# The transfers of the linear attention's first weights go behind the last tile of x

## The chip, the cores and the metric

The kernel runs on one core of one Trainium2 chip. The metric is the device time of one execution in microseconds (us): the median of the runs before is 1082.19 us, of three (1080.2 to 1083.65).

## The reference, cut to what matters

One decoder layer over 1024 tokens of width 1024, in float32:

```
h     = rmsnorm(x)
proj  = h @ w_in          # q, k, v and the indexer's iq, ik, iw of the sparse attention;
                          # q, k, v, gate rank and output gate of the linear attention
o_a   = sparse attention: per query the 256 keys with the best indexer score
        score = sum_h relu(iq_h . ik) * iw_h, then softmax over those keys
o_b   = gated linear attention in chunks of 64, RMSNorm and swish gate
x     = x + concat(o_a, o_b) @ w_out
x     = x + MoE(rmsnorm(x))   # 4 groups of 8 experts, top group, top 2 experts in it
```

Only the start of this is touched: reading x, the indexer's projection and scores, and the first part of the linear attention's projection.

## The kernel before, in words

The 1024 tokens are eight tiles of 128. TensorE works in a reduced float32 format, so each operand is held as two parts, a rounded one (hi) and what is left over (lo), and each product is three matmuls (`project_steps`, line 268). Three parts of the start matter here.

`prepare(t)` (line 287) fetches tile t of x by one transfer on SP's queue into one of three slots (tag "big", also used by the score tiles `rl` and the constants `craw`). TensorE transposes it in two halves (line 295), VectorE scales each half out of PSUM (line 298), ScalarE rounds it (line 299) and VectorE takes the rest (line 300). ScalarE squares and sums the tile (line 302) for the norm. A slot is free again when the transposes and the squares have read it.

The indexer: its weights are loaded first (`w_idx`, line 309). Projection t (24 matmuls of 312 columns) is read by ScalarE (`index_evac`, line 331), and `index_operands` (line 334) makes keys and queries of it with VectorE (lines 332 to 351), TensorE's transposes (lines 341 and 356) and ScalarE (lines 342 and 357). The scores of tile t (line 382) are evacuated by ScalarE (line 383) and added up by VectorE (line 387). The first score matmuls, of tile 2, stand in TensorE's order behind the operands of tile 3.

`load_w` (line 250) fetches weights of one group of 384 columns: four pairs of K blocks, each pair into one of three raw slots by one transfer for each piece of columns. Of each block ScalarE makes the rounded part (line 262) and GpSimd or VectorE the rest (line 263). `qkv_load(0)` has three pieces of 128 columns, so twelve transfers of 128 KB, and all its splits on GpSimd (`BY_QKV`). It is called in `filler` (line 453), whose matmuls fill TensorE's time between the score matmuls; the indexer's projections 4 to 7 come first in it, then the linear attention's q, k, v of all tiles, then `vr_load(0)` and its projection.

TensorE's order from the scoring on is the order of the program. The other engines' queues, and SP's, are ordered by a planner: it plays the program through on estimated times and issues what is ready, earlier program text first. So transfers late in the text, such as those of `qkv_load(0)`, are issued while earlier ones wait for a slot.

Of the kernel before, what the change touches and what calls it, by code (L numbers as in the profile page):

```python
# [22 lines left out]
P = 128  # L23
# [111 lines left out]
def layer(ctx, tc, x, norm1_g, w_in, q_norm_g, k_norm_g, rel_bias, gla_gate_w2, gla_gate_b, gla_out_norm_g, w_out,  # L135
          norm2_g, w_router_group, b_router_group, w_router_expert, b_router_expert, w_exp_gate, w_exp_up,
          w_exp_down, con, out):
    nc = tc.nc
    V, A, G, T = nc.vector, nc.scalar, nc.gpsimd, nc.tensor

    def f32(ap):
        return ap.bitcast(F32)
# [11 lines left out]
    def ps_tp():  # L154
        return psum.tile([P, 4, P], F32, tag="tp", name="tp", bufs=n_tp)
# [7 lines left out]
    def rsqrt(pool, y, ss, scale, bias, n, eng=None):  # L163

        e = eng or V
        u = pool.tile([P, n], F32, name="rs_u", tag=f"rs_u{n}")
        w = pool.tile([P, n], F32, name="rs_w", tag=f"rs_w{n}")
        A.activation(w, ss, AF.Ln, scale=scale, bias=eps[bias])
        A.activation(w, w, AF.Exp, scale=-0.5)
        if eng:  # L170
            e.tensor_scalar(u, ss, -0.5 * scale, -0.5 * bias, op0=OP.mult, op1=OP.add)
            e.tensor_tensor(u, u, w, op=OP.mult)
            e.tensor_tensor(u, u, w, op=OP.mult)
        elif n == 1:
            V.tensor_scalar(u, ss, -0.5 * scale, -0.5 * bias, op0=OP.mult, op1=OP.add)
            V.scalar_tensor_tensor(u, w, u, w, op0=OP.mult, op1=OP.mult)
        else:
            V.scalar_tensor_tensor(u, ss, bias / scale, w, op0=OP.add, op1=OP.mult)
            V.scalar_tensor_tensor(u, u, -0.5 * scale, w, op0=OP.mult, op1=OP.mult)
        if eng:  # L180
            e.tensor_scalar(u, u, 1.5, None, op0=OP.add)
            e.tensor_tensor(y, w, u, op=OP.mult)
        else:
            V.scalar_tensor_tensor(y, u, 1.5, w, op0=OP.add, op1=OP.mult)
# [32 lines left out]
    def two_parts(t):  # L217

        pool = hold[HOLD[t]]
        if HOLD[t] % 2:  # L220
            return [pool.tile([P, D], F32R, name="w4", tag="w4") for _ in range(2)]
        w = pool.tile([P, 2, D], F32R, name="w8", tag="w8")
        return [w[:, 0], w[:, 1]]
# [26 lines left out]
    def load_w(pieces, pool=None, width=384, by="GGGGGGGG"):  # L250
        wh, wl = [], []
        for kk in range(0, KC, 2):
            raw = wp.tile([P, 2, 384], F32, tag="wr", name="wr", bufs=3)[:, :, :width]
            o = 0
            for c, n in pieces:
                nc.sync.dma_start(raw[:, :, o:o + n],
                                  w_in[0, kk * P:(kk + 2) * P, c:c + n].rearrange("(k p) c -> p k c", p=P))
                o += n
            for k in range(2):
                a = (pool or wp).tile([P, width], F32R, tag=f"wh{kk + k}" if pool else "wh", name="wh")  # L260
                b = (pool or wp).tile([P, width], F32R, tag=f"wl{kk + k}" if pool else "wl", name="wl")
                A.activation(a, raw[:, k], AF.Copy)  # L262
                (V if by[kk + k] == "V" else G).tensor_tensor(b, raw[:, k], f32(a), op=OP.subtract)  # L263
                wh.append(a)
                wl.append(b)
        return wh, wl

    def project_steps(t, w, done, width=384):

        wh, wl = w  # L270
        ps = ps_pj()
        for k in range(KC):
            hh, hl = hT[t][0][:, k], hT[t][1][:, k]
            for i, (x_, y_) in enumerate(((hh, wh), (hh, wl), (hl, wh))):
                T.matmul(ps[:, :width], x_, y_[k], start=(k == 0 and i == 0), stop=(k == KC - 1 and i == 2))  # L275
                if k == KC - 1 and i == 2:
                    done(ps)
                yield width * 0.43

    def project(t, w, width=384):  # L280
# [2 lines left out]
            pass  # L283
        return out_[0]


    def prepare(t):
        xt = idp.tile([P, D], F32, name="xt", tag="big", bufs=3)
        nc.sync.dma_start(xt, x[0, t * P:(t + 1) * P])
        hT.append([w.rearrange("p (k t) -> p k t", k=KC) for w in two_parts(t)])  # L290
        sq = idp.tile([P, D], BF, name="sq", tag="sq", bufs=1)
        for hf in range(2):
            tp = ps_tp()
            for k in range(4):
                T.transpose(tp[:, k], xt[:, (hf * 4 + k) * P:(hf * 4 + k + 1) * P], ident)
            hi, lo = (hT[t][i][:, hf * 4:hf * 4 + 4] for i in range(2))
            xs = idp.tile([P, 4, P], F32, name="xs", tag="xs")
            V.tensor_tensor(xs, tp, g1[:, hf * 4:hf * 4 + 4, None].to_broadcast([P, 4, P]), op=OP.mult)
            A.activation(hi, xs, AF.Copy)
            V.tensor_tensor(lo, xs, f32(hi), op=OP.subtract)  # L300
        c = slice(t, t + 1)
        A.activation(sq, xt, AF.Square, accum_out=ssq[:, c])
        rsqrt(idp, rstd[:, c], ssq[:, c], 1.0 / D, EPS, 1, G)
        G.tensor_scalar(nrstd[:, c], rstd[:, c], -1.0, None, op0=OP.mult)

    with nc.allow_non_contiguous_dma("small parameter"):
        nc.sync.dma_start(g1, norm1_g[0].rearrange("(k p) -> p k", p=P))
    prepare(0)
    w_idx = load_w([(IQ, 296), (GLR, 16)], w1p, 312, "VVVVVVVV")
    prepare(1)  # L310
# [18 lines left out]
    def index_evac(t, pj):  # L329
        pr = prs[t] = idp.tile([P, 312], F32, name="pr", tag="pr")  # L330
        A.activation(pr, pj[:, :312], AF.Copy, scale=rstd[:, t:t + 1])
        V.tensor_scalar(iww[:, t], pr[:, 288:296], 0.0625, None, op0=OP.mult)

    def index_operands(t):
        pr = prs[t]
        k4 = idp.tile([P, 2, 2, 32], F32R, name="k4", tag="k4")
        ikb = pr[:, None, 256:288].to_broadcast([P, 2, 32])
        V.tensor_copy(k4[:, :, 0], ikb)
        V.tensor_tensor(k4[:, :, 1], ikb, f32(k4[:, :, 0]), op=OP.subtract)
        tp = ps_mm().rearrange("p (a t) -> p a t", a=4)  # L340
        T.transpose(tp[:, 0], f32(k4.rearrange("p a b d -> p (a b d)")), ident)
        A.activation(k4T[:, t * P:(t + 1) * P], tp[:, 0], AF.Copy)
        G.tensor_copy(glr[:, t], pr[:, 296:312])
        if t < 2:
            return
        q4 = idp.tile([P, 8, 2, 2, 32], F32R, name="q4", tag="q4", bufs=1)
        iqb = pr[:, 0:256].rearrange("p (h d) -> p h d", h=8)
        for j in range(2):
            V.tensor_copy(q4[:, :, 0, j], iqb)
        for j in range(2):  # L350
            V.tensor_tensor(q4[:, :, 1, j], iqb, f32(q4[:, :, 0, 0]), op=OP.subtract)
        q4T = idp.tile([P, 8, P], F32R, name="q4T", tag="q4T", bufs=3)
        for hf in range(2):
            tp = ps_mm().rearrange("p (a t) -> p a t", a=4)
            for h in range(4):
                T.transpose(tp[:, h], f32(q4[:, hf * 4 + h].rearrange("p a b d -> p (a b d)")), ident)
            A.activation(q4T[:, hf * 4:hf * 4 + 4], tp, AF.Copy)
        q4Ts[t] = q4T
# [36 lines left out]
    def qkv_load(p):  # L395
        c = p * P
        return load_w([(QB + c, P), (KB + c, P), (VB + 2 * c, P)], by=BY_QKV[p])

    def vr_load(p):
        c = p * P  # L400
        return load_w([(VB + 2 * c + P, P), (RG + 2 * c, 2 * P)], by=BY_VR[p])

    def evac_qkv(p, t, pj):
        gq[p, t] = gqp.tile([P, 384], F32, name="gq", tag="gq", bufs=9)
        A.activation(gq[p, t], pj[:, :384], AF.Copy, scale=rstd[:, t:t + 1])
# [17 lines left out]
    for t in range(2, NT):  # L423
        prepare(t)
# [18 lines left out]
    def filler():  # L443

        for t in range(4, NT):
            for ns in project_steps(t, w_idx, lambda ps: index_evac(t, ps), 312):
                yield ns, 0
            if t > 4:
                index_operands(t - 1)
                yield 1000, t - 1  # L450
        p1c.close()
        pools["gvp"] = p2.enter_context(tc.tile_pool(name="gvp", bufs=1, side="right"))
        w = qkv_load(0)
        for t in range(NT):
            for ns in project_steps(t, w, lambda ps: evac_qkv(0, t, ps)):
                yield ns, 0
            if t == 0:
                index_operands(NT - 1)
                yield 1000, NT - 1
        w = vr_load(0)  # L460
        for t in range(NT):
            for ns in project_steps(t, w, lambda ps: evac_vr(0, t, ps)):
                yield ns, 0
# [318 lines left out]
    w = qkv_load(1)  # L782
# [18 lines left out]
    w = vr_load(1)  # L801
# [764 lines left out]
    for i, (kind, e) in enumerate(plan):  # L1566
# [8 lines left out]
        x = xs.pop(e)  # L1575
# [19 lines left out]
    with tc.If(nov > CAP):  # L1595
# [5 lines left out]
        with tc.For_i(0, NE, 1) as e:  # L1601
# [7 lines left out]
            x, parts = {}, []  # L1609
# [51 lines left out]
```

## Time and profile before

| what | value |
|---|---|
| median of the runs | 1082.19 us |
| the profiled execution | 1076.3 us, span 1074.5 us |
| mean granted TensorE clock | 0.965 |
| busy in the span | PE 92%, DVE 71%, ACT 63%, POOL 36% |

PE is TensorE, PEld its weight loads, DVE VectorE, ACT ScalarE, POOL GpSimd; SPq is SyncE's queue, which issues transfers. The profile covers one execution. In its rows L12 is line 12 of the kernel, "wr<-in_w_in" means that tile wr is written from w_in, and x3 that three such instructions are merged. The granted clock is a share of full speed: 1.00 is 2.4 GHz and 0.50 is 1.2 GHz.

### The profile page before, as it was taken

To read this page: it belongs to the slowest core of one execution; us is meant where nothing else is said; L and a number is where in the kernel's file an instruction comes from. 1 tells how busy PE (TensorE), PEld (TensorE's weight loads), DVE (VectorE), ACT (ScalarE), POOL (GpSimd) and SP (SyncE) were. 2 spreads that over 40 slices of the span, in tenths; PEclk is the share of its full clock that TensorE was granted. 3 is DMA by queue.
4 is the path that set the end of the run, shared out by engine and by line. 5 is a ranking of instruction groups with operands and counts; after the bars stand their busy time and mean duration, and the time that the engine had idled before them with its cause. 6 is when DMAs were issued, how large, how long until landed. Compare 5 with 4: busy or idle time off the path is not lost.

```text
span 1074.5 us, 17967 instructions
## 1 busy us (share of the span) xinstructions
PE 990.3 (92%) x5839; PEld 803.9 (75%) x5839; DVE 764.2 (71%) x2037; ACT 674.0 (63%) x1662; POOL 382.2 (36%) x499
## 2 busy tenths in 40 slices
PE   7799989999998999999989999949999999999892
PEld 7789878878887988988977878836666666666561
DVE  6877898684775566767765666656887778888771
ACT  7688755365555666666755533427777777777660
POOL 4510325551413225245332201254435444443421
PEclk9899989999999999999999999968999999999996
DMA  8220202020202102012131379769999999999983
GB/s 251 81 60 1 60 1 70 11 70 21 70 11 70 38 9 65 10 51 79 58 93 48 126 255 381 292 223 286 318 317 320 326 327 324 333 316 324 341 281 46
DMA packets 83206, 170.88 MB, mean 159 GB/s; under 512 B 14856, under 2 KB 45760, under 8 KB 82976
## 3 DMA queue, kind: packets, MB, share of 16 engines
q1 hardware_dynamic: 75936, 148.01, 40.8%
q0 software_dynamic: 7168, 21.65, 9.4%
q8 instruction: 48, 0.79, 0.3%
q14 instruction: 54, 0.44, 0.1%
HBM read 148.23 MB, written 26.88 MB: 163 GB/s over the span
## 4 chain that ended last, share of the span: by engine, by line
PE 59%; DMA 14%; DVE 14%; ACT 7%; issue 3%; POOL 2%; SPq 1%; POOLq 0%; ACTq 0%; DVEq 0%
PE pj L275 19%; DMA out_dram<-y,idx 10%; PE pj L1138 8%; PE mm L1512 3%; PE po L964 3%; PE pj L1463 3%; PE pj L1464 3%; PE pj L1465 3%; PE tp L952 2%; DVE w L1386 2%; PE mm L1159 1%; PE mm L936 1%; PE tp L1473 1%; PE mm L711 1%; PE mm L935 1%
## 5 line engine op out<-in xcount | busy, mean ns | idle before, releaser
L275 PE MATMUL pj<-wh,w 128*128 128x384 f32 (+1 forms) x1152 | 322.9, 347 | 6.0 <-DVE gv L415 5.0
L275 PEld LDWEIGHTS pj<-wh,w 128*128 128x128 f32 x1152 | 211.4, 193 | 13.8 <-DVE gv L415 5.6
L1385 ACT ACTIVATE w<-w 128x512 fp32r<-128x512 f32 x320 | 192.0, 628 | 46.0 <-PE mm L1465 27.5
L1386 DVE TENSOR_TENSOR w<-w,w 128x512 fp32r<-128x512 f32 x283 | 187.2, 698 | 31.7 <-ACT w L1385 28.3
L275 PE MATMUL pj<-wl,w 128*128 128x384 f32 (+1 forms) x576 | 199.3, 346 | 1.5 <-POOL wl L263 1.1
L275 PEld LDWEIGHTS pj<-wl,w 128*128 128x128 f32 x576 | 111.8, 194 | 4.7 <-POOL wl L263 1.3
L1463 PE MATMUL pj<-w,xT 128*96 128x512 f32 x256 | 105.5, 412 | 0.6 <-ACT w L1385 0.5
L1464 PE MATMUL pj<-w,xT 128*96 128x512 f32 x256 | 101.9, 398 | 2.3 <-DVE w L1386 1.2
L1465 PE MATMUL pj<-w,xT 128*96 128x512 f32 x256 | 101.7, 397 | 0.0
L1138 PE MATMUL pj<-w,mhl 128*128 128x512 f32 x384 | 101.1, 404 | 0.0
L929 POOL TENSOR_TENSOR cb<-bt,maskb 128x256 f32<-128x256 f32 (+1 forms) x64 | 43.5, 682 | 122.1 <-DVE mx L940 103.4
L1537 POOL DMA_INDIRECT out_dram<-y,idx x30 | 52.4, 1748 | 90.0 <-ACT w L1385 53.6
L263 POOL TENSOR_TENSOR wl<-wr,wh 128x384 fp32r<-128x384 f32 x58 | 59.9, 1053 | 68.3 <-ACT wh L262 67.5
L1138 PEld LDWEIGHTS pj<-w,mhl 128*128 128x128 f32 x384 | 69.4, 189 | 12.8 <-DVE mhl L1130 0.4
L1386 POOL TENSOR_TENSOR w<-w,w 128x512 fp32r<-128x512 f32 x37 | 50.5, 1364 | 46.9 <-ACT w L1385 45.6
L1512 PE MATMUL mm<-w,hT 128*96 128x512 f32 x128 | 65.4, 592 | 0.5 <-ACT hT L1502 0.5
L943 ACT ACTIVATE z<-z,mx 128x128 f32<-128x128 f32 (+7 forms) x64 | 49.5, 774 | 22.4 <-DVE mx L940 22.0
L1463 PEld LDWEIGHTS pj<-w,xT 128*96 128x96 f32 x256 | 44.2, 173 | 15.1 <-ACT w L1385 1.3
L1465 PEld LDWEIGHTS pj<-w,xT 128*96 128x96 f32 x256 | 41.8, 163 | 18.0 <-DVE xT L1477 0.2
L1464 PEld LDWEIGHTS pj<-w,xT 128*96 128x96 f32 x256 | 41.8, 163 | 17.9 <-DVE w L1386 2.7
L1473 PEld LDWEIGHTS tp<-cf,xg 96*128 96x128 f32 x256 | 40.9, 209 | 15.8 <-issue 9.3
L1463 PE MATMUL mm<-w,hTt 128*96 128x512 f32 x64 | 50.8, 794 | 0.0
(379 smaller groups left out, 2151.7 us busy)
## 6 DMA issues: line engine op xcount, KB each, us to landing
w<-in_w_exp_gate_dram SPq DMA_DIRECT2D x64, 512.0 KB, 7.7
w<-in_w_exp_up_dram SPq DMA_DIRECT2D x64, 512.0 KB, 7.7
w<-in_w_exp_down_dram SPq DMA_DIRECT2D x64, 512.0 KB, 7.7
wr<-in_w_in_dram SPq DMA_DIRECT2D x80, 128.0 KB, 2.5
xt<-in_x_dram SPq DMA_DIRECT2D x16, 512.0 KB, 4.7
mt<-mixd SPq DMA_DIRECT2D x8, 512.0 KB, 4.3
out_dram<-xt SPq DMA_DIRECT2D x8, 512.0 KB, 3.6
h2d<-h SPq DMA_DIRECT2D x7, 528.0 KB, 5.8
```

What stands on the lines that cost most here:

```text
L263: (V if by[kk + k] == "V" else G).tensor_tensor(b, raw[:, k], f32(a), op=OP.subtract)
L275: T.matmul(ps[:, :width], x_, y_[k], start=(k == 0 and i == 0), stop=(k == KC - 1 and i == 2))
L943: A.activation(z[:, :L], z[:, :L], AF.Exp, bias=mn, scale=-1.0, accum_out=sums[:, i:i + 1])
L1138: T.matmul(ps, lhs[:, k % 4], w[k, c], start=(k == 0 and i == 0), stop=(k == KC - 1 and i == 2))
L1385: A.activation(a, u, AF.Copy)
L1386: (G if engine == "G" else V).tensor_tensor(b, u, f32(a), op=OP.subtract)
L1463: T.matmul(ps, x[0], y[0], start=first, stop=False)
L1464: T.matmul(ps, x[0], y[1], start=False, stop=False)
L1465: T.matmul(ps, x[1], y[0], start=False, stop=last)
L1473: T.transpose(tp[:, k, :n], x["xg"][:n, :D].rearrange("n (a p k) -> n a k p", a=2, k=4)[:, hf, k], ident[:n, :n])
L1512: T.matmul(pd[:n], hT0, parts[2 * hf], start=True, stop=False)
L1537: G.indirect_dma_start(out=out[0], out_offset=bass.IndirectOffsetOnAxis(ap=idx[:CAP, e:e + 1], axis=0), in_=y[:CAP], in_offset=None, compu ...
```

## The change

The instruction of each x transfer is kept in a list, and `qkv_load(0)` is traced in a block that queues its instructions on the same engine (SP, so its twelve transfers) behind the last x transfer. It is an order of issue in the planner's work: no semaphore wait is added, and the splits on ScalarE and GpSimd get no edge.

```
+    x_in = []
 ...
     def prepare(t):
         xt = idp.tile([P, D], F32, name="xt", tag="big", bufs=3)
-        nc.sync.dma_start(xt, x[0, t * P:(t + 1) * P])
+        x_in.append(nc.sync.dma_start(xt, x[0, t * P:(t + 1) * P]))
 ...
-        w = qkv_load(0)
+        with tc.issue_after(x_in[-1].ins):
+            w = qkv_load(0)
```

## Rows read from the trace of the kernel before

**Rows 1.** Windows, start:end and length in us, then busy us (instructions) by engine
```profile
core 0: us, PE busy (x) PEld busy (x) DVE busy (x) ACT busy (x) POOL busy (x), PEclk, DMA share, GB/s
20.00:30.00 10.00, 9.82 (x75) 9.56 (x73) 7.34 (x12) 10.00 (x28) 9.13 (x17) 1.00 0.92 272
30.00:40.00 10.00, 5.21 (x27) 4.01 (x27) 9.79 (x21) 5.96 (x14) 8.57 (x23) 0.71 0.47 142
...
60.00:110.00 50.00, 49.01 (x289) 46.13 (x288) 36.08 (x47) 42.43 (x101) 5.45 (x17) 1.00 0.12 33
```

**Rows 2.** The chain of waits from 24 to 42 us: start, length, what
```profile
25.32 0.83 ACT wh L262 x2
...
27.98 1.40 DVE w L300
...
38.31 1.94 PE mm L356 x8
```

**Rows 3.** Timeline of SP's queue: start, length, engine, line, operation, count
```profile
14.74 1.92 SPq L256 DMA_DIRECT2D wr<-in_w_in_dram  x4
...
23.18 1.40 SPq L256 DMA_DIRECT2D wr<-in_w_in_dram  x3
25.14 0.34 SPq L289 DMA_DIRECT2D xt<-in_x_dram  x1
...
30.73 0.42 SPq L426 DMA_DIRECT2D craw<-in_constants_dram  x1
```

**Rows 4.** Timeline of ScalarE
```profile
24.29 0.93 ACT L262 ACTIVATE wh<-wr 128x384 fp32r<-128x384 f32 x2
...
25.21 0.93 ACT L262 ACTIVATE wh<-wr 128x384 fp32r<-128x384 f32 x2
...
27.85 0.50 ACT L331 ACTIVATE pr<-pj,rstd 128x312 f32<-128x312 f32 x1
```

**Rows 5.** Timeline of TensorE
```profile
25.10 0.31 PE L275 MATMUL pj<-wh,w 128*128 128x312 f32 x1
...
39.90 0.67 PE L382 MATMUL mm<-k4T,q4T 128*128 128x384 f32 x1
...
60.68 1.04 PE L356 MATMUL mm<-cf,q 128*128 128x128 f32 x8
...
69.29 0.34 PE L275 MATMUL pj<-wh,w 128*128 128x384 f32 x1
```

**Rows 6.** Groups of VectorE by line, 27 to 41 us: count, busy us, mean ns
```profile
L300 DVE TENSOR_TENSOR w<-xs,w 128x512 fp32r<-128x512 f32 x5 | 4.1, 828 | 1.3 <-ACT w L299 1.3
...
L351 DVE TENSOR_TENSOR q<-pr,q 128x256 fp32r<-128x256 f32 x4 | 2.3, 616 | 0.0
L349 DVE CAST q<-pr 128x256 fp32r<-128x256 f32 x4 | 2.0, 543 | 0.0
```

**Rows 7.** The same groups, 44 to 62 us
```profile
L300 DVE TENSOR_TENSOR w<-xs,w 128x512 fp32r<-128x512 f32 x3 | 2.1, 686 | 0.2 <-ACT w L299 0.2
L351 DVE TENSOR_TENSOR q<-pr,q 128x256 fp32r<-128x256 f32 x4 | 1.5, 412 | 0.0
L349 DVE CAST q<-pr 128x256 fp32r<-128x256 f32 x5 | 1.3, 286 | 0.0
```

**Rows 8.** Timeline of GpSimd, first and last of four splits of the moved weights
```profile
27.81 2.43 POOL L263 TENSOR_TENSOR wl<-wr,wh 128x384 fp32r<-128x384 f32 x2
...
31.77 1.15 POOL L263 TENSOR_TENSOR wl<-wr,wh 128x384 fp32r<-128x384 f32 x1
```

**Rows 9.** Windows of other stretches, columns as in rows 1
```profile
30.00:34.40 4.40, 1.91 (x13) 1.39 (x13) 4.30 (x10) 3.06 (x7) 4.34 (x12) 0.97 0.78 242
...
40.00:44.60 4.60, 4.60 (x22) 4.53 (x21) 2.85 (x7) 2.71 (x7) 0.76 (x1) 0.53 0.00 0
...
130.00:140.00 10.00, 7.85 (x50) 7.31 (x48) 9.93 (x32) 7.05 (x15) 4.83 (x12) 1.00 0.00 1
140.00:150.00 10.00, 7.41 (x35) 7.07 (x35) 9.96 (x36) 5.36 (x10) 3.72 (x7) 0.66 0.01 2
```

**Rows 10.** Transfers into wr, from issue to landing, up to 60 us
```profile
DMA to landing us min/median/max: 2.1/4.0/5.7
```

## Prediction

> **What bounds the kernel now.** I read the page first and then four views of the first 110 us, the only stretch in which the moved transfers and what they feed run.
>
> The windows come first [rows 1]. The reader is to see that from 60 to 110 us TensorE is busy for 49.0 of 50 us, while in 30:40 it is busy for 5.2 of 10 us at a clock of 0.71. Just ahead, in 20:30, ScalarE is the full one (10.00 of 10) and VectorE still has 2.7 us free; in 30:40 VectorE is the full one (9.79). So there is a hole in TensorE's work at 30 to 40 us, and TensorE passes what is saved there on to 110 us.
>
> The chain of waits [rows 2] says who digs the hole: it runs over the ScalarE copies of the moved weights (line 262), then without a break over VectorE's splits of x and of the indexer's queries, and ends at the query transposes (line 356) behind which the first score matmul stands. That matmul starts at 39.90 [rows 5].
>
> The queue of SP [rows 3] shows where the moved transfers stand. They are twelve (four pairs of K blocks by three column pieces): the first four from 14.74, the last three from 23.18, all ahead of the last x tile, which goes at 25.14. The six of the next load (vr) follow, around the constants' load at 30.73. What the twelve feed is the copies on ScalarE [rows 4] and the splits on GpSimd [rows 8].
>
> **The change, part by part.** The statement orders only the queue: the transfers are issued behind the issue of the last x tile, not behind its landing, and nothing else gets a new wait. Its own waiter is SP. Behind the twelve on SP stand the six vr transfers and, if the planner sets it so, the constants. The copies and splits are not tied, but need the bytes.
>
> *Where the twelve go.* The last x tile needs a slot that transposes of an earlier tile free; so 25.14 stands. Twelve issues at 0.48 us (1.92 for four) [rows 3] take 5.8 us, to about 31; landing takes 2.1 to 5.7, median 4.0 us [rows 10]. The fourth pair of blocks needs a raw slot (there are three) freed by the first pair's split. I expect copies from about 30 and splits from 30.5 to 40. Nobody reads them before 69.29 [rows 5]: lateness of the weights costs nothing, with nearly 30 us of cover. If the constants' load falls behind the twelve it is up to 5.8 us later; its casts on GpSimd free a slot for score tiles. I take 0, since in the order now it is ready among them, and keep +1.5 as an upper end: the part that the saved time below would not cover.
>
> *ScalarE before 28 us.* Projection 2 of the indexer ends on TensorE at 25.41 (25.10 + 0.31) [rows 5], but ScalarE reads it at 27.85, since two pairs of copies stand before it, at 24.29 and 25.21 [rows 4]. A pair takes 0.83 us of the queue (the chain's figure [rows 2]; the 0.93 of the timeline holds an overlap). Without them: 1.7 us earlier. The ends are 0 (the planner puts other work there) and 2.4 (27.85 less 25.41). VectorE has the room to use it: 2.7 us free [rows 1]. I take **-1.7**. The eight copies come back between 30 and 44.6, 8 x 0.42 = 3.3 us, where ScalarE is idle for 1.3 us (3.06 of 4.4 busy) and 1.9 us (2.71 of 4.6) in the first and the last stretch [rows 9]: 0, at worst one pair ahead of a needed copy, +0.8.
>
> *VectorE against GpSimd.* Three kinds of VectorE instructions take longer in 27 to 41 us [rows 6] than in 44 to 62 [rows 7], where no split runs: line 300 828 against 686 ns (5 x 0.142 = 0.71 us), line 351 616 against 412 (4 x 0.204 = 0.82), line 349 543 against 286 (4 x 0.257 = 1.03). That is 2.6 us in the chain itself. In the stretch GpSimd runs five splits, four of them of the moved weights (27.81 to 32.9) [rows 8], and behind them two casts of about a split's length together; four parts of six, 1.7 us, leave. They don't leave for good: splits that restart at about 30.5 meet the rest of this very chain. If the chain now ends at about 36 in place of 38.3, two or three splits fall in, 2.5 x 0.43 (2.6 over six) = 1.1 us. Net **-0.6**. The ends: -1.7 (all fall behind the chain) and +4.1 (all eight fall in, each at the worst that one line 300 lost, 1.40 [rows 2] less 0.69, 0.72 x 8 = 5.8, less 1.7). The splits that fall into the scoring from 40 on meet a VectorE that is busy for 2.85 of 4.6 us beside a full TensorE [rows 9]: 0.
>
> The Trainium skill ("SBUF — State Buffer", section "Who interferes with whom") says that a VectorE instruction with two SBUF inputs and a GpSimd instruction that reads SBUF exclude each other, and the later one waits for the whole of the earlier. By that rule each of the eight splits could cost up to its own 1.2 us here, and the part would be up to 9.7 - 1.7 = +8 us; the means of [rows 6] show 0.43 a split, since not every instruction meets one. Line 300 at 1.40 us in [rows 2] agrees with the rule, and it speaks against this change; rival 1 is its milder form.
>
> *The clock.* After 30:34.4, with TensorE busy for 1.91 of 4.4 us, the granted clock falls to its lower level (1.2 GHz) and is back at 44.6 [rows 9]. On the path that costs 0.9 us in the query transposes (1.94 [rows 2] against 1.04 at full clock [rows 5]) and 2.3 in the 4.6 us up to 44.6, together 3.2. With operands 2 ready some 3 us earlier, their transposes move up and the second half of the next x tile's (0.6 us) into that stretch, 2.5 of 4.4 us busy by my estimate: between this hole, where the clock fell, and 130:140, where it held at 7.85 of 10; at 7.41 in 140:150 it fell [rows 9]. The ends are 0 and -3.2; I take the middle, **-1.6**, as a slow stretch that is shorter by half.
>
> The x tiles ahead of the weights land up to some 2 us earlier. Tiles 5 to 7 are read by TensorE long after they land, so: 0.
>
> Sum: -1.7 - 0.6 - 1.6 = -3.9 us. The profiled execution takes 1076.3 us (its span 1074.5 and 1.8 around it), so 1072.4 in such an execution. The runs shown have a median of 1082.19, 5.9 above the profiled one; off that median the forecast is **1078.3 us**. Behind 110 us all work hangs on the scores, and I carry the gain to the end in full.
>
> **Rivals.**
>
> 1. *The splits eat the gain.* VectorE, not ScalarE, is the busy engine in 30:40, and the splits move from 21-36 to 30-40. With six of them in the chain, 6 x 0.43 = 2.6 us return; -1.7 - 1.7 + 2.6 = -0.8, and the clock falls all the same: 1081.4, no change. For it: the timing worked out above. Against it: operands 2 are through before the splits begin.
>
> 2. *Slower: ScalarE stands before late weights.* ScalarE takes its instructions in order. If the planner sets a pair of copies among the score evacuations by its own clock, and the fourth pair's transfer, which waits for a split that VectorE in turn delays, is still under way, ScalarE stands for a landing: up to 4.0 us [rows 10], and the scores with it. It decides from the point where the fourth pair's copies stand in the queue ahead of the first evacuations, at 36 to 42 us. Price 4.0, with the +2.6 of the splits, less the 1.7 + 1.7: +3.2; with the worst splits (+4.1) +6.4. Time 1085 to 1089, say 1086.5. For it: three raw slots only. Against it: now ScalarE hardly waits for a transfer.
>
> 3. *The hole closes.* All splits fall behind the chain and the clock holds: -1.7 - 1.7 - 3.2 = -6.6, 1075.6.
>
> 4. *The change is an order, no wait, and changes nothing that matters*, because the planner replans the later queues by its own clock and gains or loses there: the stretch 140:150 [rows 9] shows one place where the clock takes up to 3.4 us (0.34 of 10). Lost once more, with the -0.8 of rival 1: 1084.8.
>
> **How the numbers follow.** What a measurement of this kernel tells from no change is about 0.3%, 3.2 us. Forecast (about -3.9, from 1075.5 to 1080): 0.34; rival 3: 0.12; rival 1: 0.32; rival 2: 0.16; rival 4, lost: 0.06. So faster 0.46, same 0.32, slower 0.22. The range leaves out the far half of rival 3's gains and the worst of rival 2: 1073 to 1087.
>
> **What would show it.** In the changed profile the twelve line 256 issues stand behind the last x tile, with no line 262 copies of 384 columns on ScalarE before 28 us; the reading of projection 2 follows at about 26; line 349 and 351 for that tile run at 0.29 and 0.41 us; the first score matmul starts at 36 to 37.5 in place of 39.90. The clock's low stretch is shorter than 10 us or absent. The prediction is wrong if the first score matmul comes at 39 or later, if ScalarE waits for the weights' landing, or if a saving at 60 us is not there at 110.

## The result, and the profile after

The changed kernel takes 1088.18 us (median of 20 runs, 1083.6 to 1094.75) where the kernel before, beside it on the same chip, takes 1082.92: a ratio of 1.0063, 95% interval 1.0042 to 1.0084, so some 6.8 us slower by the ratio (the medians lie 5.3 us apart). The forecast was 1078.3 us, faster, with a range up to 1087. (The ratios leave out executions more than 1.5% above the fastest of their kernel, one or none of most kernels but three of the twelve of e9 below; the medians hold all.)

The profiled execution has a span of 1082.1 us, the one of before 1074.5. In the changed kernel's trace the lines behind the edit stand 2 or 3 further down: 300 is 302, 331 is 333, 382 is 384, 1385 is 1388, 1520 is 1523, 1537 is 1540.

The start first. The windows, as in [rows 1]:

```profile
20.00:30.00 10.00, 10.00 (x78) 9.99 (x77) 7.36 (x20) 7.85 (x22) 6.70 (x25) 1.00 0.50 171
30.00:40.00 10.00, 5.25 (x33) 4.49 (x31) 8.30 (x13) 8.06 (x21) 8.97 (x15) 0.76 0.73 192
...
60.00:110.00 50.00, 49.10 (x286) 46.27 (x285) 36.08 (x58) 42.34 (x100) 5.40 (x19) 1.00 0.11 32
```

ScalarE has left 20:30 (10.00 busy before, 7.85 now) and come back in 30:40 (5.96, now 8.06); TensorE's hole in 30:40 is as deep as it was (5.21, now 5.25), and VectorE, full there before (9.79), now stands idle for 1.7 us (8.30). SP's queue, to hold against [rows 3]:

```profile
17.55 8.49 SPq L291 DMA_DIRECT2D xt<-in_x_dram  x3
26.09 4.02 SPq L256 DMA_DIRECT2D wr<-in_w_in_dram  x8
30.22 0.39 SPq L428 DMA_DIRECT2D craw<-in_constants_dram  x1
30.66 13.51 SPq L256 DMA_DIRECT2D wr<-in_w_in_dram  x10
```

The edit does what it says: the twelve go behind the last x tile, the first eight from 26.09, and the constants slip in among them. ScalarE, against [rows 4]; the last bracket is idle time and what ended it:

```profile
25.23 1.06 ACT L304 ACTIVATE sq<-xt 128x1024 bf16<-128x1024 f32 x1 [1.34 <-DMA xt<-in_x_dram]
...
26.68 0.50 ACT L333 ACTIVATE pr<-pj,rstd 128x312 f32<-128x312 f32 x1
...
29.28 1.06 ACT L304 ACTIVATE sq<-xt 128x1024 bf16<-128x1024 f32 x1 [0.81 <-DMA xt<-in_x_dram]
...
31.01 0.53 ACT L262 ACTIVATE wh<-wr 128x384 fp32r<-128x384 f32 x1 [0.58 <-DMA wr<-in_w_in_dram]
...
32.04 0.61 ACT L301 ACTIVATE w<-xs 128x512 fp32r<-128x512 f32 x1
```

Projection 2 is read at 26.68 (27.85 before), but ScalarE, freed of the copies, now stands for tiles of x, and then for the weights: line 301 at 32.04 had its input by 30.5, but it stands in the queue behind the 0.58 us wait and two copies. VectorE, its timeline and its groups against [rows 6], and GpSimd, against [rows 8]:

```profile
32.69 1.43 DVE L302 TENSOR_TENSOR w<-xs,w 128x512 fp32r<-128x512 f32 x1 [1.60 <-ACT w L301]
...
36.58 1.58 DVE L353 TENSOR_TENSOR q<-pr,q 128x256 fp32r<-128x256 f32 x2
```

```profile
L302 DVE TENSOR_TENSOR w<-xs,w 128x512 fp32r<-128x512 f32 x5 | 5.0, 995 | 1.6 <-ACT w L301 1.6
...
L353 DVE TENSOR_TENSOR q<-pr,q 128x256 fp32r<-128x256 f32 x4 | 2.3, 622 | 0.0
L351 DVE CAST q<-pr 128x256 fp32r<-128x256 f32 x4 | 1.8, 486 | 0.0
```

```profile
31.62 1.96 POOL L263 TENSOR_TENSOR wl<-wr,wh 128x384 fp32r<-128x384 f32 x2 [0.81 <-ACT wh L262]
...
34.31 1.05 POOL L263 TENSOR_TENSOR wl<-wr,wh 128x384 fp32r<-128x384 f32 x1
...
36.55 0.99 POOL L263 TENSOR_TENSOR wl<-wr,wh 128x384 fp32r<-128x384 f32 x1
...
37.86 5.40 POOL L263 TENSOR_TENSOR wl<-wr,wh 128x384 fp32r<-128x384 f32 x4
```

All eight splits now run between 31.6 and 43.3, seven of them begun before the first score matmul, over the very chain they had partly left, and line 302 takes 995 ns where line 300 took 828. VectorE waits 1.60 us for the delayed line 301. TensorE, against [rows 5]:

```profile
38.31 1.94 PE L358 MATMUL mm<-cf,q 128*128 128x128 f32 x8 [0.82 <-ACT wh L262]
...
41.19 0.67 PE L384 MATMUL mm<-k4T,q4T 128*128 128x384 f32 x1
...
67.91 0.34 PE L275 MATMUL pj<-wh,w 128*128 128x384 f32 x1
```

The query transposes start when they did in [rows 2]. The bracket names ScalarE's copy, because that ended last before them, but they read what VectorE's line 353 writes: it ends at 38.16, within 0.01 us of where it ended before, and they start 0.15 us later, as before. The first score matmul is later (39.90 before), behind four transposes of x that wait for VectorE; the first matmul of 384 columns is 1.38 us earlier (69.29 before): the clock's low stretch is 6.8 us long in this execution, from 35.2, in place of 10.2.

So the start does not hold the loss. To find it I took the start of the same matmul in both traces (matmuls matched in order by line and operands), the execution after less the one before:

| near (us) | 40 | 68 | 355 to 550 | 570 | 735 | 800 | 812 to 835 | 985 | 1031 |
|---|---|---|---|---|---|---|---|---|---|
| after - before (us) | +1.3 | -1.4 | -2.0 to -2.1 | -0.9 | +0.6 | +1.1 | +3.4 to +6.8 | +2.9 | +8.7 |

The lead holds for 500 us. Near 555 and 705 to 735 it is lost, 2.7 us in all, though the queues have the same order there; near 555 the clock's low stretch is 6.8 us long in this execution and 3.4 in the one of before, and near 705 it is 30.7 and 27.3. The loss itself, 8.1 us, is made in the loop over the experts (from about 735 us), and most plainly in its last turns, at 990 to 1031. I looked at each queue's order of instructions in the two programs. Behind the start they are the same until the expert loop; there TensorE and SP keep the program's order, but the planner has put ScalarE, VectorE and GpSimd into another one: some thirty instructions have changed places with neighbours. In letters, ScalarE from about 1000 us (w: a weight copy, line 1385; s: the silu, 1491; Y: the evacuation of half of y, 1520; x: of half of the next expert's xT, 1476; h, H: of hT, 1501 and 1502):

```
before   wwswwwwYxwwwwxhH  wwsYwwwwwwwwxwwxhH  swwwwY ...
after    wwsYwwwwwwwwxxwwhH  sYwwwwwwwwxwwxhH  swwwwY ...
```

In the common turn near 1000 us four weight copies stand ahead of Y and four behind. I call a turn with Y ahead of all eight a late turn. The kernel before has one, the changed kernel two. ScalarE of the kernel before, the common turn and then its late one:

```profile
1001.48 0.38 ACT L1491 ACTIVATE sl<-pj 96x256 f32<-96x256 f32 x1 [0.52 <-PE pj L1465]
1001.76 2.18 ACT L1385 ACTIVATE w<-w 128x512 fp32r<-128x512 f32 x4
1003.85 0.58 ACT L1520 ACTIVATE y<-mm 96x512 f32<-96x512 f32 x1
...
1014.86 0.59 ACT L1520 ACTIVATE y<-mm 96x512 f32<-96x512 f32 x1 [2.07 <-DMA out_dram<-y,idx]
1015.36 4.26 ACT L1385 ACTIVATE w<-w 128x512 fp32r<-128x512 f32 x8
```

y has one buffer, so Y waits until the scatter of the expert before (line 1537, adding y into the output) has landed. In the common turn the four copies cover that. In the late turn ScalarE stands for it, 2.07 us, and all eight copies come after. (In the changed kernel's first late turn it is 2.04 us; in its second, Y waits 1.17 us for TensorE instead.) GpSimd of the changed kernel, and TensorE's waits there:

```profile
1010.12 2.32 POOL L1540 DMA_INDIRECT out_dram<-y,idx  x1 [3.43 <-ACT w L1388]
1012.00 1.73 POOL L1389 TENSOR_TENSOR w<-w,w 128x512 fp32r<-128x512 f32 x1
...
1023.41 4.14 POOL L1540 DMA_INDIRECT out_dram<-y,idx  x1 [3.64 <-ACT w L1388]
1027.08 1.75 POOL L1389 TENSOR_TENSOR w<-w,w 128x512 fp32r<-128x512 f32 x1
```

```profile
1013.78 0.48 PE L1467 MATMUL pj<-w,xT 128*96 128x512 f32 x1 [1.02 <-POOL w L1389]
...
1028.89 0.74 PE L1467 MATMUL pj<-w,xT 128*96 128x512 f32 x1 [3.54 <-POOL w L1389]
```

GpSimd's one split a turn (line 1389) waits for its weight copy, and for the scatter now ahead of it, and TensorE waits for the split. The kernel before waits there once, for 1.05 us.

### The profile page after: what moved, and what is told of

Read it like the earlier page. It is cut to its first block, busy times and chain, and to the rows that moved or that the text cites. A ratio compares the mean times of both kernels' runs of the same rounds, so it can differ in the third digit from the quotient of the medians.

```text
span 1082.1 us, 17966 instructions
## 1 busy us (share of the span) xinstructions
PE 994.9 (92%) x5839; PEld 807.1 (75%) x5839; DVE 766.3 (71%) x2037; ACT 675.7 (62%) x1662; POOL 385.0 (36%) x499
## 5 line engine op out<-in xcount | busy, mean ns | idle before, releaser
L1389 DVE TENSOR_TENSOR w<-w,w 128x512 fp32r<-128x512 f32 x283 | 188.6, 700 | 36.8 <-ACT w L1388 33.2
L1467 PE MATMUL pj<-w,xT 128*96 128x512 f32 x256 | 103.5, 404 | 6.2 <-POOL w L1389 4.6
L1466 PE MATMUL pj<-w,xT 128*96 128x512 f32 x256 | 106.7, 417 | 0.9 <-ACT w L1388 0.5
L1468 PE MATMUL pj<-w,xT 128*96 128x512 f32 x256 | 102.7, 401 | 0.0
L1533 POOL DMA_INDIRECT xg<-h2d,idxf x29 | 33.9, 1170 | 48.5 <-PE tp L1501 27.9
```

The lines of the kernel that those rows point to most:

```text
L1389: (G if engine == "G" else V).tensor_tensor(b, u, f32(a), op=OP.subtract)
L1466: T.matmul(ps, x[0], y[0], start=first, stop=False)
L1467: T.matmul(ps, x[0], y[1], start=False, stop=False)
L1468: T.matmul(ps, x[1], y[0], start=False, stop=last)
```

## The experiments

All but three of the runs (e3, e6 and e7) hold the expert loop's three queues in a chosen order. After the loop is traced, each instruction of a list is queued behind the one before it in the list, without a semaphore; the lists are the queues of the kernel before, of the changed kernel, or mixtures:

```
+    by = {i.name: i for i in tc.nc.cur_bb.bb.instructions}
+    for text in PINNED.values():
+        names = [n for n in map("I-{}".format, text.split()) if n in by]
+        for a, b in zip(names, names[1:]):
+            tc.add_manual_dep(by[b], a, mybir.DependencyInfo(mybir.DependencyClass.NoSync, mybir.DependencyReason.DATA),
+                              reason="pin")
```

**e1_early_only**: the changed kernel with the expert loop in the order of before.

> The change at the start is kept; in the expert loop the queues of ScalarE, VectorE and GpSimd are held in the order of the kernel before. Theory A (the loss is made in the expert loop by the planner's new order there): the saving of the first 60 us comes through, -1.5 to -2 us against before, so 0.998 to 1.000, and no 6 us are lost between 800 and 1030 us. Theory B (the order is innocent; the loop is slow because it starts at another moment against the transfers and the clock): it stays as slow as the changed kernel, 1.005 or more.

1083.28 us against 1081.65, ratio 1.002 (0.9986 to 1.0054). By the medians it lies 8.6 us under e3, which has the changed kernel's order and ran beside it, as theory A has it; the saving that the theory expected on top does not show.

**e2_expert_order_only**: the kernel before, no edit at the start, with the changed kernel's expert loop order.

> The start is that of the kernel before; in the expert loop the queues of ScalarE, VectorE and GpSimd are held in the order that the changed kernel has there. Theory A: slower than before by 7 to 9 us (the 6.8 of the changed kernel and the 1.5 to 2 that it saves at the start), 1.006 to 1.008. Theory B: as before, 0.999 to 1.001.

1087.64 us, ratio 1.0074 (1.0036 to 1.0112). The loss comes without the edit, by the order alone. Its trace loses 10 us between 1000 and 1031 against the one of before.

**e3_after_again**: the changed kernel with its line numbers kept as before, so that traces can be laid side by side.

> The changed kernel once more beside the other two, on the same chip (its statements put on the lines of the kernel before). Both theories: 1.004 to 1.008, some 6.8 us above before, and 1.5 us ahead of before at 60 us.

1091.87 us (6 runs), ratio 1.0109 (1.0062 to 1.0156): the loss is that of the changed kernel again.

Then I asked which of the swaps does it; the first suspect was the scatter ahead of the split.

**e4_one_swap**: before, with only that swap on GpSimd.

```
 POOL before: ... gate, split, scatter, gate ...
 POOL e4:     ... gate, scatter, split, gate ...
```

> The kernel before, with the expert loop's queues of ScalarE, VectorE and GpSimd held in the order of before, except that in GpSimd's queue one scatter of y (L1537) stands before the split of the next weight tile (L1386), as it does in the changed kernel. Theory A1 (this one swap makes the loss of the expert loop): slower by 6 to 8 us, ratio 1.005 to 1.008, the scatter near 1004 us lasts over 4 us beside VectorE's splits, and TensorE waits twice for about 3.5 us on GpSimd's w between 1000 and 1030. Rival A2 (the y evacuations against w copies on ScalarE and VectorE make it): ratio 0.999 to 1.001 and no such waits.

1085.02 us against 1081.19, ratio 1.0023 (1.0 to 1.0047). The waits came as expected (4.6 us on GpSimd's w in two, the longest 3.5), in a profiled execution that was the longest of its twelve; the time did not go up by 6. So the swap has a price, but it is not the whole.

**e5_swap_undone**: the changed kernel in its own order, with that swap alone taken back.

> The changed kernel, all three queues of the expert loop held in its own order, except that on GpSimd the split stands before the scatter again. Theory A1: ratio 0.998 to 1.002, and the loss at 1000 to 1030 us is gone (about 1 us of wait on GpSimd's w there in place of 4.6). Rival A2: ratio stays at 1.005 or more.

1089.89 us (6 runs), ratio 1.0109 (1.0066 to 1.0153). The theory that this one swap makes the loss falls. GpSimd in e5's first late turn shows why:

```profile
1010.93 4.58 POOL L1386 TENSOR_TENSOR w<-w,w 128x512 fp32r<-128x512 f32 x1 [3.38 <-ACT w L1385]
1015.69 1.45 POOL L1537 DMA_INDIRECT out_dram<-y,idx  x1 [0.17 <-issue]
```

The split is first again, but still waits 3.38 us for ScalarE's copy, and then takes 4.58 us beside seven splits that VectorE runs without a break. What makes it late, I took from this, is the place of Y on ScalarE. The runs that follow move that turn as a whole, VectorE's half of y and the two xT with it, so Y alone is not shown to be the cause.

**e8_late_turn** and **e9_early_swaps**: the start of before with one half of the changed order each, from 1000 us on (the second late turn) or up to there.

> The kernel before, expert loop held in its own order except for one expert late in the loop (from 1000 us on): there ScalarE, VectorE and GpSimd take the changed kernel's order, in which ScalarE's evacuation of y (L1520) stands ahead of all eight weight copies (L1385), the evacuation of the next expert's xT (L1476) behind all eight, and the scatter ahead of GpSimd's split. Theory A3 (this expert's turn makes the loss): slower by 5 to 8 us, ratio 1.005 to 1.008, with 4 to 6 us of TensorE's waits on GpSimd's w and ScalarE's xT at 1000 to 1030. Rival A4 (the earlier swaps, from 765 us, make it by the scatters that the y evacuation waits for): within 0.998 to 1.002 here.

> The reverse: the changed kernel's order up to that expert (765 to 1000 us), and the order of before from there on, on the start of before. Theory A3: 0.998 to 1.002. Rival A4: 1.005 to 1.008.

e8: 1085.88 us against 1082.81, ratio 1.0013 (0.9984 to 1.0042). e9: 1083.97, ratio 0.9993 (0.9957 to 1.0028). The early swaps alone do nothing that can be measured; the late turn alone did less than expected, though its profiled execution (1091.41 us, the longest of its twelve) lost 8 us at 1000 to 1031.

**e10_next_turn_mended** and **e11_mended_with_change**: the late turn that the kernel before has of its own is put like the others, on either start.

```
 ACT before  wwsYwwwwwwwwxwwxhH        POOL before  scatter, split
 ACT e10     wwswwwwYxwwwwwwxhH        POOL e10     split, scatter
```

VectorE's half of y and its xT move in the same way.

> The order of before has one such turn of its own, at the expert after that one (y's evacuation ahead of eight weight copies, near 1015 us). Here that turn is put like those of the experts ahead of it: four weight copies, y, the next xT, then the other four, and GpSimd's split ahead of the scatter; nothing else changes. Theory A3: as the second such turn costs 5 to 8 us, taking away the first gives 3 to 6 us: ratio 0.994 to 0.997. Rival: the weights of the last experts are late anyway, 0.999 to 1.001.

> The changed start with the mended order of the run before this one. Theory A3: the start gives nothing or up to 2 us, so 0.993 to 0.997, at or a little under the run before. Rival as there: 0.998 to 1.002.

e10: 1077.81 us against 1082.81, ratio 0.9954 (0.9928 to 0.998), faster than before. e11: 1078.21, ratio 0.9961 (0.993 to 0.9992). With the order held, the change at the start makes no difference that can be measured.

**e12 to e15**: the halves again, now on the changed start: its own early order with no late turn (e12), before's early order with two late turns (e13), its own early order with one (e14), its own order throughout (e15).

> The changed kernel, its own order up to 1000 us, and from there on the mended order, in which no expert's y stands ahead of eight weight copies. If the late turns make the loss (A3): as the mended kernels, 0.994 to 0.998. If the early swaps make it (A4): 1.003 or more. If only both together do (A5): 0.995 to 0.999.

> The changed kernel, in before's order up to 1000 us, and its own two late turns behind that. A3: 1.004 to 1.009. A4: 0.998 to 1.002. A5: 0.999 to 1.003, clearly below the whole order.

> The changed kernel, its own order up to 1000 us and before's behind that (one late turn). A3: 0.998 to 1.002. A4: 1.004 to 1.009. A5: 0.998 to 1.002.

> The changed kernel with its own order held throughout (nothing else differs from the changed kernel): all theories 1.005 to 1.011, as the changed kernel itself; near 1.000 would say that the loss hangs on the chip and not on the order.

| run | early part | late turns | median us (before 1082.37) | ratio and interval |
|---|---|---|---|---|
| e12 | own | 0 | 1077.52 | 0.9943 (0.9914 to 0.9972) |
| e14 | own | 1 | 1084.23 | 0.9999 (0.9968 to 1.003) |
| e13 | as before | 2 | 1086.14 | 1.0012 (0.9982 to 1.0042) |
| e15 | own | 2 | 1089.06 | 1.0037 (1.0006 to 1.0068) |

With the early part the same, each late turn costs: 0 to 1 turn +6.7 us, 1 to 2 turns +4.8 us, by the medians; on the start of before 0 to 1 is +5.0 (e10 against before) and 1 to 2 is +3.1 (e8). e12 and e14 came out as the late turns alone would have it (A3). e13 lies where A5 put it, under the 1.004 of A3, and e15 lies under the 1.005 that all theories expected, though its interval reaches it.

The traces separate more plainly than the times. Matched with the one trace of before as in the table above, the stretch from 983 to 1033 us is 1.0 to 2.1 us shorter in the three without a late turn (e10, e11, e12), up to 1.3 longer in those with one (e1, e9, e14; with the swap of e4 5.3), and 5.8 to 11.0 longer in the seven with two, whichever the early part.

TensorE's windows from 1000 to 1030 in e12, in the kernel before and in the changed kernel, columns as in [rows 1]:

```profile
1000.00:1010.00 10.00, 9.38 (x41) 5.77 (x39) 7.12 (x14) 6.49 (x15) 4.70 (x4) 1.00 1.01 340
1010.00:1020.00 10.00, 9.45 (x42) 6.24 (x43) 7.08 (x14) 6.43 (x15) 3.77 (x3) 1.00 1.01 328
1020.00:1030.00 10.00, 9.80 (x44) 6.46 (x43) 9.09 (x17) 8.52 (x19) 2.26 (x2) 1.00 0.97 312
```

```profile
1000.00:1010.00 10.00, 9.33 (x42) 5.83 (x40) 7.12 (x14) 6.47 (x13) 4.58 (x4) 1.00 0.99 330
1010.00:1020.00 10.00, 8.73 (x36) 5.04 (x34) 7.49 (x13) 7.33 (x17) 3.17 (x3) 1.00 1.01 362
1020.00:1030.00 10.00, 8.93 (x39) 5.97 (x39) 8.45 (x15) 6.51 (x15) 2.02 (x2) 1.00 1.00 324
```

```profile
1000.00:1010.00 10.00, 8.87 (x38) 5.22 (x37) 6.84 (x13) 6.82 (x15) 2.08 (x3) 1.00 1.04 338
1010.00:1020.00 10.00, 8.60 (x39) 5.80 (x40) 8.36 (x12) 5.27 (x13) 3.79 (x3) 1.00 1.02 340
1020.00:1030.00 10.00, 6.06 (x23) 3.38 (x22) 5.96 (x10) 5.65 (x11) 5.42 (x2) 0.92 0.98 351
```

TensorE is busy for 28.6, 27.0 and 23.5 of the 30 us with no, one and two late turns, and only with two does the clock give way (0.92). For GpSimd's w TensorE does not wait at all in e12 from 985 to 1035, and 7.0 us, in two waits, in e15.

**e6_no_splits_after** and **e7_no_splits_before**: both starts without the eight splits of the moved weights (the rounded part stands in for the rest, so that part of the computation is left out). The planner orders the later loop anew, so only the start is read (the one execution of each took 1090.1 and 1079.1 us).

```
-  (V if by[kk + k] == "V" else G).tensor_tensor(b, raw[:, k], f32(a), op=OP.subtract)
 ...
-  wl.append(b)
 ...
+  if lo: (V if by[kk + k] == "V" else G).tensor_tensor(b, raw[:, k], f32(a), op=OP.subtract)
 ...
+  wl.append(b if lo else a)
 ...
+  return load_w([(QB + c, P), (KB + c, P), (VB + 2 * c, P)], by=BY_QKV[p], lo=p > 0)
```

> The changed kernel without GpSimd's eight splits of the linear attention's first weights (the rounded part is used in place of the rest, so that the products differ); only the first 60 us are read. Theory S1 (the splits that moved to 31 to 44 us slow VectorE's copies of x, and so eat the start's gain): the first score matmul comes at 36 to 38 us in place of 41.2. Rival S2 (the splits don't matter): it stays at 40 to 41.

> The kernel before without the same eight splits (products differ in the same way); only the first 60 us are read. Theory S1: its first score matmul comes at 38 to 39 us in place of 39.9, later than that of the run with the changed start without splits. Rival S2: 39.9 as before, and the same as there.

The first score matmul of e6 and of e7:

```profile
38.01 0.67 PE L382 MATMUL mm<-k4T,q4T 128*128 128x384 f32 x1
```

```profile
37.72 0.67 PE L382 MATMUL mm<-k4T,q4T 128*128 128x384 f32 x1
```

Without the splits this matmul comes 3.2 us earlier (41.19 to 38.01) in the changed start and 2.2 (39.90 to 37.72) in the one of before, one execution each. How far that is the splits' doing the other traces tell: the matmul starts at 39.16 to 40.84 in the six that have the start of before with its splits, so 37.72 lies outside; with the changed start it is 37.95 to 41.84 in nine, so 38.01 alone proves nothing. I had expected e7 to come at 38 to 39, behind e6, and it came ahead; at the first 384-column matmul e6 is ahead (64.91 against 66.97).

How sure any start is, the fifteen other traces tell together. The first 384-column matmul starts at 66.05 to 69.62 us, mean 67.83, in the nine with the changed start, and at 66.49 to 69.29, mean 68.14, in the six with the start of before. The edit is worth 0.3 us there, a tenth of what one start varies by. The first score matmul, by the same traces, is 0.6 us later with the edit (means 40.57 and 39.95).

## Why the prediction was wrong

**ScalarE before 28 us (-1.7).** Right in kind: the copies left, the read of projection 2 moved by 1.2 us, to 26.68, and VectorE was through with its operands at 29.3 in place of 33.2, even more than the "some 3 us" that were forecast. The rest went into a new wait of 1.34 us on a tile of x.

**VectorE against GpSimd (-0.6).** The three lines that the prediction counted lose more, not less: by the same count 5 x 0.309 + 4 x 0.210 + 4 x 0.200 = 3.2 us against the uncontended means of [rows 7], in place of 2.6. But VectorE's other instructions between 27 and 41 us, which it left out, lose less: the same 23 instructions in all fill 12.2 us of its timeline where they filled 12.8. So the term as a whole came out at -0.6, by luck, for the timing under it was wrong: I had let two or three splits fall into the rest of the chain, and seven of the eight began before the first score matmul. That is the timing of rival 1, and 0.3 us gained over fifteen traces is near its -0.8 for the start; but the splits alone did not take the gain, as the late weights below show. The rule of the Trainium skill ("SBUF — State Buffer", "Who interferes with whom") that was weighed there held in direction; the most that the prediction worked out from it, 1.2 us a split, did not come.

**The clock (-1.6).** The profiled execution agrees (a low stretch of 6.8 us in place of 10.2), but by itself that shows nothing: the stretch is 3.4 us in e2 and e9 with the start of before, 10.2 in e8 and in e13, and absent at the start of e14 with the changed one. It varies from execution to execution by more than the edit could move it. The comparison behind the middle value does not hold either: the clock fell at 139.9 us, behind the stretch 130:140 with its 7.85 of 10 that the prediction took for one where it held.

**Late weights, and the copies that come back (0, at worst +0.8).** This term ate the gain up to the first score matmul. Nothing on TensorE read the weights late, but ScalarE did: it stood 0.58 us for their landing, made two copies, and only then the line 301 that VectorE needed, so VectorE stood idle for 1.60 us (32.69). Start for start, VectorE begins this work 0.8 us earlier than before, idles 1.6 us, saves 0.6 us of its own time, and is done 0.2 us later (40.97 and 40.75). It is no accident of one execution: in all nine traces with the changed start ScalarE waits 0.3 to 0.9 us for that landing and VectorE 0.6 to 2.2 us behind it, and in the six with the start of before neither wait is there. This is the mechanism of rival 2, with copies ahead of a split of x in place of score evacuations, and in small. That its time, 1085 to 1089, holds the measured one is luck: the loss was not made there. Two of the prediction's own signs of being wrong came, a first score matmul at 39 or later (41.19) and a ScalarE that waits for the weights; both spoke of the start alone.

**"Behind 110 us all work hangs on the scores, and I carry the gain to the end in full."** This is the step that failed, and it made the time come out slower; with the start alone there is no change that can be measured (e10 and e11). The small gain was carried, as the positions show, some 500 us far. But the order of the queues is not fixed behind 110 us. The planner plays the program through on its own times, and with the shift at the start it put other instructions first in the expert loop, 700 us later. (That the order changed is read from the two programs; how the planner came to it was not looked into.) Rival 4 had this mechanism, with a chance of 0.06 and a guess at the clock near 140 us as its place. The place was the turn of one expert with the evacuation of y ahead of eight weight copies, in the first such turn in front of a scatter still under way (2.04 us). e2 shows that this order alone, without the edit, gives the loss (1.0074), and e1 that the edit without it gives none that can be measured (1.002). e12, on the changed start, shows that with the late turns away the kernel is faster than before.

**What stays open.** The second late turn alone gives 1.0013 and 1.0012 (medians +3.1 and +3.8 us), the early swaps alone 0.9993 and 0.9999, the whole order 1.0037 to 1.0109. The intervals allow the parts to add up, but don't show it. Whether the early swaps add 2 to 3 us beside a late turn is not settled. They do cost where they stand: from 800 to 819 us the eight traces with the changed early order lose 2.1 to 4.4 us on the one of before (in the changed kernel's, Y waits 2.75 and 3.46 us for scatters there), and the other six with before's order at most 0.3. But by 983 us the two groups have lost about the same since 800 (means 3.8 and 4.9 us), and within each group executions differ by more than that. Nor was it tried which other part of a late turn costs, beside the scatter of e4 and e5: Y, VectorE's half of y, or the two xT.

**What came of it.** e12 and e10 beat both kernels, at 1077.52 and 1077.81 us: what they share, no turn near 1000 us with y ahead of all eight weight copies, is worth 5 us over before; the edit at the start is worth nothing beside it.

## What to carry to other kernels

Where a planner orders the queues, a small change anywhere can reorder a loop far behind it. So compare the queues' orders of the two programs before the gain is carried to the end, and hold the order fixed where the change itself is to be timed. An evacuation into a tile with a single buffer waits for that tile's last transfer: work that others need, such as weight copies, belongs ahead of it in the queue. And work taken out of a hole by delaying its input comes back; ask onto which engine's chain, and what stands behind it in that engine's queue when the input is late.

## What the hardware showed beyond that

Issuing one scatter from GpSimd took 1.42 to 2.33 us in all turns of the kernel before, but 4.14 us in the changed kernel's second late turn (4.12 to 4.14 there in all seven kernels that have two) and 4.72 us in the first late turn of e8, here with the split behind it:

```profile
1013.44 4.72 POOL L1537 DMA_INDIRECT out_dram<-y,idx  x1 [3.43 <-DVE w L1386]
1017.72 1.73 POOL L1386 TENSOR_TENSOR w<-w,w 128x512 fp32r<-128x512 f32 x1
```

VectorE in the same stretch:

```profile
1012.55 4.29 DVE L1386 TENSOR_TENSOR w<-w,w 128x512 fp32r<-128x512 f32 x7
```

They end at 1018.2 and 1016.8, so the issue seems to wait for the seven two-input splits, which run without a break at 0.68 us each. In the late turn of the kernel before, the issue and GpSimd's own split both run beside the seven:

```profile
1017.01 2.32 POOL L1537 DMA_INDIRECT out_dram<-y,idx  x1 [3.44 <-ACT w L1385]
1018.87 1.75 POOL L1386 TENSOR_TENSOR w<-w,w 128x512 fp32r<-128x512 f32 x1
```

```profile
1016.13 6.26 DVE L1386 TENSOR_TENSOR w<-w,w 128x512 fp32r<-128x512 f32 x7
```

The seven take 6.26 us in place of 4.29, but one by one a single of them is long, 2.48 us from 1018.70, and it runs beside GpSimd's split; the other six take 0.68 to 0.69 us, those beside the issue too. So where the two overlap it is the issue that yields: in the seventeen traces it takes 1.42 to 2.33 us with up to four of VectorE's splits beside it, and 4.12 to 4.74 us in the fifteen places with six or seven, while no such split is over 0.8 us long beside an issue alone. That was read from the traces and not tried on its own. The Trainium skill ("SBUF — State Buffer", "Who interferes with whom") infers that such a VectorE instruction does not hold up the writing of a GpSimd transfer's descriptors. The rows of e8, and those of the other traces, speak against that. For GpSimd's own arithmetic the same section says that it excludes such instructions, and e5's split of 4.58 us agrees: it ends at 1015.5, 1.1 us behind a run of seven on VectorE (1010.1 to 1014.4).
